# Attention's products in source order on TensorE, V products a block later, projections spread over a pair: a hybrid decoder trunk on one core

## The chip, the cores and the metric

One core of one Trainium2 chip runs the whole kernel in one launch. The metric is the device time of an execution in microseconds; lower is better. Line numbers L... are those of the kernel before, unless a row comes from the changed kernel, where the same lines stand ten to twelve lines further down.

## What is computed

Two layers over 512 positions of width 1024, in float32:

```python
h = rmsnorm(x) * (1 + scale1(c)) + shift1(c)
proj = h @ w_in                      # q, k, v of 3 head groups
# A: 4 heads, two softmax maps each, a = p0 - lam * p1
# B: 6 heads, mixture of 3 dilated windows; C: 6 heads with forget bias
x = x + gate1(c) * (concat(heads) @ w_out)
h = rmsnorm(x) * (1 + scale2(c)) + shift2(c)
u, g = split(h @ w_up)
x = x + gate2(c) * ((silu(conv3(g)) * u) @ w_down)
```

A final rmsnorm follows. scale, shift and gate come from `silu(c) @ w_mod`. Sixteen heads of width 64 make eight pairs.

## The kernel before, in words

**Precision.** Each operand of a large product is held as two parts of a fast matmul type: hi, a copy rounded by ScalarE (ACT), and lo, the rest, taken by VectorE (DVE). A product is three matmuls, hi x hi, hi x lo and lo x hi (`mm3`, L264). Weights are loaded in chunks by SyncE's DMA queue (SP) and split in the same way (L174 on ACT, L186 on DVE); `W.pump` does this one chunk ahead.

**Attention** (`layer_attn`) runs over 64 blocks in each layer: eight pairs in the order B0 B1 A0 C0 A1 C1 B2 C2 (pairs 0 to 7 here), two heads each, four blocks of 128 queries. Block i of a head sees 128 (i + 1) keys. For one block:

- `emit_S`: the score products s (two accumulating matmuls for kinds B and C; kind A has two maps, each in a PSUM buffer of its own, and the pool `ps_s` has two buffers);
- `emit_max` (DVE, L654) adds the mask and takes the row maximum nm; `emit_exp` (ACT, L667); for kind A `emit_norm` combines the two maps;
- `emit_T`: transposes of e into pt (L695); `emit_hi` (ACT, L714) and `emit_lo` (DVE, L719) split them into pth and ptl, once for blocks 0 and 1 of a head together and once each for blocks 2 and 3;
- `emit_PV`: the V products po (L741, L742), four matmuls after block 1 of a head and eight after block 3. `head_post` then forms the head's output: it copies po, divides by the sums through transposes pr, and for kind A normalises with a product sbps.

The loop over b at L819 issues, per step, the transposes of block b - 2, the maximum and exponential of b, the score of b + 1 and the V product of b - 2.

**Fills.** Between these, `fill` puts other products: the q and k projections of the next pair (`qk_chunk`, 24 matmuls of 512 columns each), half a chunk of V projection (`v_half`, 48 matmuls of 256 columns, pairs 0 to 5), and in pair 7 the output projection (`out_part`). `fills` holds their cost per pair; a step of the loop asks for the shares f1, f2 and f3 of it at three places. With 0.06 + 0.055 + 0.055 = 0.17 a step, a pair's fills are used up in about six of its eight blocks. q comes first, then k, then V.

**From a projection to scores.** `qk_post` turns the PSUM result into the tiles qk that the score products read. Kind C copies straight from PSUM (`stack_gen`: L436, L447 on ACT, L433 on DVE). Kind B first applies the rotary tables: a copy qf (ACT, L469), two DMAs that swap neighbouring rows into sw (L471, L472), three DVE operations (L475, L477, L479), then the stack copies with one more ACT copy (L449). Kind A rotates likewise, splits qf into hi (in sw, L254) and lo (in qf, L256), and twelve DMAs on SP's queue (L490) put 32-row pieces into four qk tiles; the first head needs the first six. These steps are generators that `tick` advances one step at a time, with each piece of a fill.

**What orders the instructions.** The source order gives each instruction a priority; a scheduler then places the instructions on each engine by when it expects their inputs. So PE's order before differs from the source: where a score product is not expected to be ready, later products go ahead of it. At run time each engine works through its own list in order.

Of the kernel before, what the change touches and what calls it, by code (L numbers as in the profile page):

```python
# [30 lines left out]
def kernel(  # L31
# [27 lines left out]
    V, A, T, G = nc.vector, nc.scalar, nc.tensor, nc.gpsimd  # L59
# [25 lines left out]
    def tick():  # L85
        for g in list(aux):
            if next(g, StopIteration) is StopIteration:
                aux.remove(g)
# [6 lines left out]
    ident = cst[:, C_ID:C_ID + 128]  # L95
# [20 lines left out]
    for l in range(DEPTH):  # L116
# [16 lines left out]
        for m in range(KC):  # L133
            for b in range(0, FC, 8):
                n = min(8, FC - b)
# [123 lines left out]
    def pair_tiles(pool, tag, name):  # L259
        hi = pool.tile([128, SEQ], F32R, tag=tag, name=name + "h")  # L260
        lo = pool.tile([128, SEQ], F32R, tag=tag, name=name + "l")
        return hi, lo

    def mm3(ps, w, rhs, first, last, c=slice(0, SEQ)):  # L264
        T.matmul(ps[:, c], w[0], rhs[0][:, c], start=first, stop=False, skip_group_check=True)  # L265
        T.matmul(ps[:, c], w[0], rhs[1][:, c], start=False, stop=False, skip_group_check=True)  # L266
        T.matmul(ps[:, c], w[1], rhs[0][:, c], start=False, stop=last, skip_group_check=True)  # L267

    def feat_q(ps, w, act, first=True, last=True, k0=0):
        n = len(act)  # L270
# [108 lines left out]
    def layer_attn(l, ap, mods, st, rt0):  # L379
        h = st.h  # L380
# [5 lines left out]
        def v_post(q, cols):  # L386
            vv = vvs[q]
            for t in range(2):
                src = [cols(2 * t + b).rearrange("p (h d) -> p h d", h=4) for b in range(2)]
                for b in range(2):  # L390
                    A.activation(out=vv[:, 2 * t + b, :, 0:64], in_=src[b], func=AF.Copy)
                yield
                for b in range(2):
                    V.tensor_tensor(out=vv[:, 2 * t + b, :, 64:128], in0=src[b],
                                    in1=vv[:, 2 * t + b, :, 0:64].bitcast(F32), op=ALU.subtract)
                yield
# [4 lines left out]
        def v_half(q, half):  # L401
            nb, n = (1, VZ) if q == 0 else (2, 256)
            if half == 0:
                pools = {"m": (mm, "mm"), "t": (ps_t, "pt"), "o": (ps_o, "o")}
                vps[q] = [pools[c][0].tile([128, SEQ], F32, tag=pools[c][1], name="vps")
                          for c in ("otmt" if q == 0 else "mm")]
            pss = vps[q]
            w = W.use()
            for j in range(4):
                k = 4 * half + j  # L410
                wc = w(n * j, n * j + n)
                for tb in range(4):
                    b = slice(128 * tb, 128 * tb + 128)
                    d = pss[tb // nb][:, 256 * (tb % nb):256 * (tb % nb) + n]
                    go = k == 0 and tb % nb == 0
                    en = k == KC - 1
                    T.matmul(d, h[k][0][:, b], wc[0], start=go, stop=False, skip_group_check=True)
                    T.matmul(d, h[k][0][:, b], wc[1], start=False, stop=False, skip_group_check=True)
                    T.matmul(d, h[k][1][:, b], wc[0], start=False, stop=en, skip_group_check=True)
                W.pump(j)  # L420
                yield
            if half == 1:
                if q == 0:
                    for tb in range(4):
                        V.tensor_tensor(out=z[:, tb, :], in0=pss[tb][:, 256:VZ], in1=fb[:, l, :], op=ALU.add)
                vvs[q] = ap.tile([128, 4, 4, 128], F32R, tag="vv", name="vv", bufs=2)
                aux.append(v_post(q, lambda tb: pss[tb // nb][:, 256 * (tb % nb):256 * (tb % nb) + 256]))
# [86 lines left out]
        def after(g):  # L514
            while True:
                with tc.issue_after(anchor[0]), tc.issue_after(anchor[1]):
                    if next(g, StopIteration) is StopIteration:
                        return
                yield
# [104 lines left out]
        def emit_S(b):  # L624
            idx, kind, hh, i = blocks[b]
            q, k = qks[idx, 0], qks[idx, 1]
            n = 128 * (i + 1)
            qb = slice(128 * i, 128 * i + 128)
            if kind != "A":
                s = ps_s.tile([128, SEQ], F32, tag="s", name="s")  # L630
                T.matmul(s[:, 0:n], q[hh][:, qb], k[hh][:, 0:n], start=True, stop=False)
                if kind == "B":
                    T.matmul(s[:, 0:n], q[hh][:, qb], k[2 + hh][:, 0:n], start=False, stop=True)  # L633
                else:
                    T.matmul(s[:, 0:n], q[2 + hh][0:68, qb], k[2 + hh][0:68, 0:n], start=False, stop=True)
                S[b] = [s]
                return
            res = []
            for mp in range(2):
                s = ps_s.tile([128, SEQ], F32, tag="s", name="s")  # L640
                T.matmul(s[:, 0:n], q[2 * hh + mp][0:96, qb], k[2 * hh + mp][0:96, 0:n], start=True, stop=True)
                res.append(s)
            S[b] = res

# [41 lines left out]
        def emit_T(b):  # L686
            i = blocks[b][3]
            e = E.pop(b)
            if i == 1:
                pt = pts[b - 1][0]  # L690
            else:
                pt = ps_t.tile([128, SEQ], F32, tag="pt", name="pt")
            for j in range(i + 1):
                c = 128 * (i + j) if i < 2 else 128 * j
                T.transpose(pt[:, c:c + 128], e[:, 128 * j:128 * j + 128], ident)  # L695
            if i % 2 == 0:
                n = (384, 1024)[i // 2]
                pts["cur"] = tuple(ap.tile([128, n], F32R, tag="%s%d" % (t, i), name=t, bufs=1) for t in ("pth", "ptl"))
            pts[b] = (pt,) + pts["cur"]
# [21 lines left out]
        def emit_PV(b):  # L721
            idx, kind, hh, i = blocks[b]
            if i % 2 == 0:
                return
            half = i // 2
            _, pth, ptl = pts.pop(b)
            pts.pop(b - 1)
            if half == 0:
                po_t["cur"] = ps_o.tile([128, SEQ], F32, tag="o", name="po")
            po = po_t["cur"]  # L730
            while running("v_post"):
                tick()
            vv = vvs[idx // 2]
            hd = 2 * (idx % 2) + hh
            nj = 2 * half + 2
            for j in range(nj):
                c0 = 128 if j == nj - 1 else 0
                oc = slice(256 * half + c0, 256 * half + 256)
                a = 256 * j if half == 0 else 256 * j + c0
                pc = slice(a, a + 256 - c0)  # L740
                T.matmul(po[:, oc], vv[:, j, hd, :], pth[:, pc], start=(j == 0), stop=False, skip_group_check=True)  # L741
                T.matmul(po[:, oc], vv[:, j, hd, :], ptl[:, pc], start=False, stop=(j == nj - 1), skip_group_check=True)  # L742
            if half == 1:
                aux.append(head_post(idx, kind, hh, po))

# [56 lines left out]
        nb = len(blocks)  # L802

        def running(name):
            return any(g.__name__ == name for g in aux)

        def ready(b):
# [5 lines left out]
            while not done(idx):  # L813
                tick()

        emit_S(0)
        lag = 2
        f1, f2, f3 = 0.06, 0.055, 0.055
        for b in range(nb + lag):  # L819
            idx = blocks[min(b, nb - 1)][0]  # L820
            while idx and fills[idx - 1][0]:
                fill(idx - 1, 1.0)
            p = b - lag
            if l == 0 and b == 10:
                with tc.issue_after(anchor[0]), tc.issue_after(anchor[1]):
                    prep()
            if b == 3:
                aux.append(after(fz_post()))
            if p >= 0:
                emit_T(p)  # L830
            if b < nb:
                emit_max(b)
            if p >= 0:
                emit_hi(p)
            fill(idx, f1)
            if b < nb:
                emit_exp(b)
            if p >= 0:
                emit_lo(p)
            fill(idx, f2)  # L840
            if b + 1 < nb:
                ready(b + 1)
                emit_S(b + 1)
            if b < nb:
                emit_norm(b)
            fill(idx, f3)
            if p >= 0:
                emit_PV(p)
            ms, mr = 4, 3.2
            if b >= ms:  # L850
                for _ in range(int((b - ms + 1) * mr) - int((b - ms) * mr)):
                    next(modg, None)
        aux.append(modg)
        for idx in range(8):
            while fills[idx][0]:
# [137 lines left out]
    with ExitStack():  # L993
# [7 lines left out]
        with tc.tile_pool(name="start", bufs=1) as stp:  # L1001
# [19 lines left out]
            for op in STARTUP:  # L1021
# [4 lines left out]
                else:  # L1026
                    k = int(op[1])
# [162 lines left out]
```

## Time and profile before

| what | value |
|---|---|
| median of three executions | 1338.51 us (1336.86 to 1346.54) |
| profiled execution | 1337.11 us, span 1335.3 us, mean granted clock 0.989 |
| layer 0 attention, blocks | about 60 to 305 us |
| layer 0 MLP | about 310 to 700 us |
| layer 1 attention, blocks | about 700 to 910 us |
| layer 1 MLP and final norm | about 915 to 1335 us |

How to read it: PE is the matmul unit and PEld its weight loads. A row of a timeline has the start and the duration in us; matmuls are pipelined, so a row's duration is longer than the distance to the next start. A row of the table by stretches has the stretch, its length, the busy time of PE, PEld, DVE, ACT and POOL with counts, the granted clock of TensorE, the DMA share and GB/s. A row of the table of waits has who waited for whom, the sum in us, the number and the longest. A row of groups ends with the busy time, the mean ns of one, and the idle time of the engine before them with what ended most of it.

### The profile page before, as it was taken

To read this page: it belongs to the slowest core of one execution; us is meant where nothing else is said; L and a number is where in the kernel's file an instruction comes from. 1 tells how busy PE (TensorE), PEld (TensorE's weight loads), DVE (VectorE), ACT (ScalarE), POOL (GpSimd) and SP (SyncE) were. 2 spreads that over 40 slices of the span, in tenths; PEclk is the share of its full clock that TensorE was granted. 3 is DMA by queue.
4 is the path that set the end of the run, shared out by engine and by line. 5 is a ranking of instruction groups with operands and counts; after the bars stand their busy time and mean duration, and the time that the engine had idled before them with its cause. 6 is when DMAs were issued, how large, how long until landed. Compare 5 with 4: busy or idle time off the path is not lost.

```text
span 1335.3 us, 18235 instructions
## 1 busy us (share of the span) xinstructions
PE 1278.1 (96%) x6568; PEld 1058.2 (79%) x6568; DVE 868.8 (65%) x1733; ACT 671.5 (50%) x1254; POOL 94.1 (7%) x64
## 2 busy tenths in 40 slices
PE   4899999999999999999999999999999999999997
PEld 1688787778888878888898888878878888888886
DVE  6888989868888886433347787875754444443232
ACT  5577888954433333322336677785543333333231
POOL 5232423400000000000000000000000000000000
PEclk8899999999999999999999999999999999999999
DMA  9445553432777775333333234212133333332331
GB/s 373 146 136 158 165 156 129 137 113 82 249 251 256 247 253 152 91 97 93 113 113 94 85 108 128 78 57 89 49 108 95 97 94 96 95 91 87 103 99 63
DMA packets 68127, 174.44 MB, mean 131 GB/s; under 512 B 9410, under 2 KB 11730, under 8 KB 68036
## 3 DMA queue, kind: packets, MB, share of 16 engines
q1 hardware_dynamic: 66884, 172.16, 40.9%
q8 instruction: 52, 0.85, 0.3%
q10 hardware_dynamic: 1088, 1.05, 0.2%
q14 instruction: 39, 0.32, 0.1%
q0 software_dynamic: 64, 0.06, 0.0%
HBM read 159.41 MB, written 2.10 MB: 121 GB/s over the span
## 4 chain that ended last, share of the span: by engine, by line
PE 59%; DVE 9%; DMA 6%; ACT 4%; issue 2%; SPq 0%; DVEq 0%; ACTq 0%
PE dps L265 6%; PE dps L267 6%; PE dps L266 6%; DMA rawm<-in_wmod_dram 5%; PE pg L266 4%; PE pu L265 4%; PE pg L267 4%; PE pu L267 4%; PE pu L266 4%; PE pg L265 4%; DVE wlo L186 2%; PE ops L265 2%; PE ops L266 2%; PE ops L267 2%; DVE rawm L228 2%
## 5 line engine op out<-in xcount | busy, mean ns | idle before, releaser
L186 DVE TENSOR_TENSOR wlo<-raww,whi 128x1024 fp32r<-128x1024 f32 (+3 forms) x188 | 228.2, 1214 | 232.0 <-ACT whi L174 227.8
L174 ACT ACTIVATE whi<-raww 128x1024 fp32r<-128x1024 f32 (+3 forms) x188 | 194.5, 1035 | 335.8 <-PE dps L266 137.8
L266 PE MATMUL pg<-hl,whi 128*128 128x512 f32 (+1 forms) x368 | 143.1, 389 | 0.5 <-DVE hl L314 0.2
L265 PE MATMUL pg<-hh,whi 128*128 128x512 f32 (+1 forms) x368 | 141.5, 385 | 1.6 <-ACT whi L174 1.6
L265 PE MATMUL pu<-hh,whi 128*128 128x512 f32 (+1 forms) x368 | 142.3, 387 | 0.0
L267 PE MATMUL pg<-hh,wlo 128*128 128x512 f32 (+1 forms) x368 | 141.0, 383 | 1.1 <-DVE wlo L186 1.1
L267 PE MATMUL pu<-hh,wlo 128*128 128x512 f32 (+1 forms) x368 | 140.6, 382 | 0.1
L266 PE MATMUL pu<-hl,whi 128*128 128x512 f32 (+1 forms) x368 | 140.7, 382 | 0.0
L265 PE MATMUL dps<-mh,whi 128*128 128x512 f32 x308 | 121.5, 394 | 0.0
L267 PE MATMUL dps<-mh,wlo 128*128 128x512 f32 x308 | 121.5, 394 | 0.0
L266 PE MATMUL dps<-ml,whi 128*128 128x512 f32 x308 | 121.2, 393 | 0.0
L667 ACT ACTIVATE e<-e,nm 128x256 f32<-128x256 f32 (+3 forms) x160 | 88.9, 556 | 33.9 <-DVE nm L654 30.6
L265 PE MATMUL qkps<-hh,whi 128*128 128x512 f32 x224 | 95.7, 427 | 1.0 <-ACT qf L469 0.7
L907 ACT ACTIVATE y<-y 128x512 f32<-128x512 f32 x44 | 27.8, 632 | 127.0 <-DVE y L904 117.0
L266 PE MATMUL qkps<-hl,whi 128*128 128x512 f32 x224 | 89.5, 400 | 0.0
L267 PE MATMUL qkps<-hh,wlo 128*128 128x512 f32 x224 | 89.4, 399 | 0.0
L654 DVE CUSTOM_DVE_ANT_0 e<-s,cst 128x256 f32<-128x256 f32 (+3 forms) x160 | 76.3, 481 | 17.7 <-PE s L633 6.2
L267 PEld LDWEIGHTS pg<-hh,wlo 128*128 128x128 f32 x368 | 69.0, 188 | 17.0 <-DVE wlo L186 2.4
L221 POOL TENSOR_TENSOR rawm<-rawm,scb 128x512 f32<-128x512 f32 x48 | 71.2, 1492 | 160.1 <-DMA rawm<-in_wmod_dram 115.6
L267 PEld LDWEIGHTS pu<-hh,wlo 128*128 128x128 f32 x368 | 69.1, 188 | 16.7 <-DVE wlo L186 1.2
L266 PEld LDWEIGHTS pg<-hl,whi 128*128 128x128 f32 x368 | 69.0, 188 | 16.6 <-DVE hl L314 2.0
L265 PEld LDWEIGHTS pg<-hh,whi 128*128 128x128 f32 x368 | 69.1, 188 | 16.0 <-ACT whi L174 2.0
(183 smaller groups left out, 2820.2 us busy)
## 6 DMA issues: line engine op xcount, KB each, us to landing
raww<-in_wup_dram SPq DMA_DIRECT2D x88, 512.0 KB
rawm<-in_wmod_dram SPq DMA_DIRECT2D x160, 256.0 KB
raww<-in_wqk_dram SPq DMA_DIRECT2D x32, 512.0 KB
raww<-in_wdown_dram SPq DMA_DIRECT2D x32, 512.0 KB
mu<-in_wmod_dram SPq DMA_DIRECT2D x16, 512.0 KB
raww<-in_wout_dram SPq DMA_DIRECT2D x16, 448.0 KB
raww<-in_wv_dram SPq DMA_DIRECT2D x12, 512.0 KB
raww<-in_wdown_dram SPq DMA_DIRECT2D x16, 384.0 KB
```

Of the source, the lines that this page charges most:

```text
L174: A.activation(out=h[:, 0:m], in_=self.raw[i][:, c:c + m], func=AF.Copy)
L186: V.tensor_tensor(out=lo[:, 0:m], in0=raw[:, c:c + m], in1=h[:, 0:m].bitcast(F32), op=ALU.subtract)
L221: G.tensor_tensor(out=raw, in0=raw, in1=scb[:, 512 * half:512 * half + 512], op=ALU.mult)
L228: V.tensor_tensor_reduce(out=raw, in0=raw, in1=scb[:, 512 * half:512 * half + 512], scale=1.0, scalar=prev, op0=ALU.mult, op1=ALU.add, acc ...
L265: T.matmul(ps[:, c], w[0], rhs[0][:, c], start=first, stop=False, skip_group_check=True)
L266: T.matmul(ps[:, c], w[0], rhs[1][:, c], start=False, stop=False, skip_group_check=True)
L267: T.matmul(ps[:, c], w[1], rhs[0][:, c], start=False, stop=last, skip_group_check=True)
L654: anchor[0] = V.tensor_tensor_reduce(out=e[:, 0:n], in0=s[:, 0:n], in1=cst[:, mask + SEQ - n:mask + SEQ], scale=-scale, scalar=3e38, op0=A ...
L667: anchor[1] = A.activation(out=e[:, 0:n], in_=e[:, 0:n], func=AF.Exp, bias=nm, scale=-1.0, accum_out=den).ins
L907: last_silu[0] = A.activation(out=y, in_=y, func=AF.Silu).ins
```

## The change

Three edits, all in `layer_attn` and its helpers:

1. Within the block loop each matmul and transpose of projections, scores, transposes and V products is tied behind the one issued before it (`tc.issue_after`), so PE gets them in source order. `head_post` and `fz_post` still issue their few matmuls untied.
2. `emit_PV` is called for block p - 1 instead of p: one block later; the loop runs one step longer.
3. f1, f2, f3 are 0.045, 0.04, 0.04, together 0.125: one eighth of a pair's fills per block.

```diff
+    row = [False, None]
+
+    def pe(ins):
+        with (tc.issue_after(row[1]) if row[0] and row[1] else ExitStack()):
+            r = ins()
+        row[1] = r.ins
+
+    def mmul(*a, **k):
+        pe(lambda: T.matmul(*a, **k))
+
     def mm3(ps, w, rhs, first, last, c=slice(0, SEQ)):
-        T.matmul(ps[:, c], w[0], rhs[0][:, c], start=first, stop=False, skip_group_check=True)
+        mmul(ps[:, c], w[0], rhs[0][:, c], start=first, stop=False, skip_group_check=True)
...
-                T.transpose(pt[:, c:c + 128], e[:, 128 * j:128 * j + 128], ident)
+                pe(lambda: T.transpose(pt[:, c:c + 128], e[:, 128 * j:128 * j + 128], ident))
...
-        f1, f2, f3 = 0.06, 0.055, 0.055
-        for b in range(nb + lag):
+        f1, f2, f3 = 0.045, 0.04, 0.04
+        row[0] = True
+        for b in range(nb + lag + 1):
...
-            if p >= 0:
+            if 0 <= p < nb:
                 emit_T(p)
...
-            if p >= 0:
-                emit_PV(p)
+            if p >= 1:
+                emit_PV(p - 1)
...
+        row[0] = False
```

The other `T.matmul` calls of `v_half`, `emit_S` and `emit_PV` become `mmul` in the same way.

**Order on PE, start of pair 2 (kind A) in layer 0.** s is a score product, vps the V projection, qkps the q and k projections, pt transposes. Before:

```order
L265 MATMUL qkps<-hh,whi 128x512
L266 MATMUL qkps<-hl,whi 128x512
L267 MATMUL qkps<-hh,wlo 128x512
L641 MATMUL s<-qk 128x128
L265 MATMUL qkps<-hh,whi 128x512
L266 MATMUL qkps<-hl,whi 128x512
L267 MATMUL qkps<-hh,wlo 128x512
```

Now:

```order
L272 MATMUL po<-ptl,vv 128x128
L705 MATMUL pt<-cst,e 128x128 x2
L272 MATMUL vps<-whi,hh 128x256
L272 MATMUL vps<-wlo,hh 128x256
L272 MATMUL vps<-whi,hl 128x256
...
L272 MATMUL s<-qk 128x128 x2
L705 MATMUL pt<-cst,e 128x128 x3
L272 MATMUL qkps<-hh,whi 128x512
```

Before, fifteen qkps matmuls of the next pair's projection and other work stood ahead of the pair's first score product. Now the k projection of this pair is followed by 48 vps matmuls, the scores of blocks 6 and 7 of the pair before, eight po matmuls and three transposes, and then by the score product; the next pair's qkps come behind it. Pairs 1 and 3 to 6 of both layers start in the same way (pair 1 with the pf products and four transposes of the forget bias among the rows).

**Order on ACT, the same place, now.** qf and sw are the k side of pair 2, vv<-vps copies the V projection out, pth is the split of the transposes.

```order
L479 ACTIVATE qf<-qkps 128x512
L677 ACTIVATE e,dens<-e,nm 128x384
L224 ACTIVATE rawm,mq<-rawm 128x512
L677 ACTIVATE e,dens<-e,nm 128x512
L224 ACTIVATE rawm,mq<-rawm 128x512
L759 ACTIVATE ot<-po 64x512
L724 ACTIVATE pth<-pt 128x384
L401 ACTIVATE vv<-vps 128x4x64
L254 ACTIVATE sw<-qf 128x512
```

The split sw<-qf stands behind pth, which reads the two transposes above, and behind a vv copy of the last V projection. At pair 4 of both layers the same two stand ahead of it; at pair 2 of layer 1 only pth does. At pair 6 the stack copies stand behind pth in the same way.

**Order on PE, start of pair 7 (kind C) in layer 0, now.** The qkps here are the k projection of pair 7 itself; ops is the output projection.

```order
L705 MATMUL pt<-cst,e 128x128 x2
L272 MATMUL qkps<-hh,whi 128x512
L272 MATMUL qkps<-hl,whi 128x512
L272 MATMUL qkps<-hh,wlo 128x512
L272 MATMUL qkps<-hh,whi 128x512
L272 MATMUL qkps<-hl,whi 128x512
L272 MATMUL qkps<-hh,wlo 128x512
L272 MATMUL s<-qk 128x128 x2
L705 MATMUL pt<-cst,e 128x128 x3
L272 MATMUL ops<-oh,whi 128x512
```

Before, fourteen other PE rows (V products, the last score of pair 6, transposes, two ops matmuls) stood between the last k projection and that score product; now none does.

More of the change, by code (lines that the diff above doesn't have):

```diff
@@ L262, in pair_tiles @@
         return hi, lo
+    row = [False, None]
[5 more added lines that the diff above has]
+        pe(lambda: T.matmul(*a, **k))
     def mm3(ps, w, rhs, first, last, c=slice(0, SEQ)):
-        T.matmul(ps[:, c], w[0], rhs[0][:, c], start=first, stop=False, skip_group_check=True)
-        T.matmul(ps[:, c], w[0], rhs[1][:, c], start=False, stop=False, skip_group_check=True)
-        T.matmul(ps[:, c], w[1], rhs[0][:, c], start=False, stop=last, skip_group_check=True)
+        mmul(ps[:, c], w[0], rhs[0][:, c], start=first, stop=False, skip_group_check=True)
+        mmul(ps[:, c], w[0], rhs[1][:, c], start=False, stop=False, skip_group_check=True)
+        mmul(ps[:, c], w[1], rhs[0][:, c], start=False, stop=last, skip_group_check=True)
     def feat_q(ps, w, act, first=True, last=True, k0=0):
@@ L416, in v_half @@
                     en = k == KC - 1
-                    T.matmul(d, h[k][0][:, b], wc[0], start=go, stop=False, skip_group_check=True)
-                    T.matmul(d, h[k][0][:, b], wc[1], start=False, stop=False, skip_group_check=True)
-                    T.matmul(d, h[k][1][:, b], wc[0], start=False, stop=en, skip_group_check=True)
+                    mmul(d, h[k][0][:, b], wc[0], start=go, stop=False, skip_group_check=True)
+                    mmul(d, h[k][0][:, b], wc[1], start=False, stop=False, skip_group_check=True)
+                    mmul(d, h[k][1][:, b], wc[0], start=False, stop=en, skip_group_check=True)
                 W.pump(j)
@@ L630, in emit_S @@
                 s = ps_s.tile([128, SEQ], F32, tag="s", name="s")
-                T.matmul(s[:, 0:n], q[hh][:, qb], k[hh][:, 0:n], start=True, stop=False)
+                mmul(s[:, 0:n], q[hh][:, qb], k[hh][:, 0:n], start=True, stop=False)
                 if kind == "B":
-                    T.matmul(s[:, 0:n], q[hh][:, qb], k[2 + hh][:, 0:n], start=False, stop=True)
+                    mmul(s[:, 0:n], q[hh][:, qb], k[2 + hh][:, 0:n], start=False, stop=True)
                 else:
-                    T.matmul(s[:, 0:n], q[2 + hh][0:68, qb], k[2 + hh][0:68, 0:n], start=False, stop=True)
+                    mmul(s[:, 0:n], q[2 + hh][0:68, qb], k[2 + hh][0:68, 0:n], start=False, stop=True)
                 S[b] = [s]
@@ L640, in emit_S @@
                 s = ps_s.tile([128, SEQ], F32, tag="s", name="s")
-                T.matmul(s[:, 0:n], q[2 * hh + mp][0:96, qb], k[2 * hh + mp][0:96, 0:n], start=True, stop=True)
+                mmul(s[:, 0:n], q[2 * hh + mp][0:96, qb], k[2 * hh + mp][0:96, 0:n], start=True, stop=True)
                 res.append(s)
@@ L740, in emit_PV @@
                 pc = slice(a, a + 256 - c0)
-                T.matmul(po[:, oc], vv[:, j, hd, :], pth[:, pc], start=(j == 0), stop=False, skip_group_check=True)
-                T.matmul(po[:, oc], vv[:, j, hd, :], ptl[:, pc], start=False, stop=(j == nj - 1), skip_group_check=True)
+                mmul(po[:, oc], vv[:, j, hd, :], pth[:, pc], start=(j == 0), stop=False, skip_group_check=True)
+                mmul(po[:, oc], vv[:, j, hd, :], ptl[:, pc], start=False, stop=(j == nj - 1), skip_group_check=True)
             if half == 1:
@@ L832, in layer_attn @@
                 emit_max(b)
-            if p >= 0:
+            if 0 <= p < nb:
                 emit_hi(p)
@@ L837, in layer_attn @@
                 emit_exp(b)
-            if p >= 0:
+            if 0 <= p < nb:
                 emit_lo(p)
@@ L846, in layer_attn @@
             fill(idx, f3)
-            if p >= 0:
-                emit_PV(p)
+            if p >= 1:
+                emit_PV(p - 1)
             ms, mr = 4, 3.2
```

## The prediction

> **What bounds the kernel now.** I read the page's busy line first, then a table by stretches for the two attention stages (layer 0: 60 to 305 us, layer 1: 700 to 910), then the table of waits inside them.
>
> ```profile
> span 1335.3 us, 18235 instructions
> PE 1278.1 (96%) x6568; PEld 1058.2 (79%) x6568; DVE 868.8 (65%) x1733; ACT 671.5 (50%) x1254; POOL 94.1 (7%) x64
> ```
> ```profile
> 60.00:305.00 245.00, 230.29 (x1357) 193.13 (x1357) 208.37 (x500) 194.69 (x459) 71.36 (x49) 0.99 0.46 146
> 700.00:910.00 210.00, 205.60 (x1269) 176.06 (x1268) 166.79 (x422) 153.46 (x344) 0.00 (x0) 0.99 0.29 87
> ```
>
> PE sets the end. No matmul is added or removed, so only the time in which PE stands still can change, and the edit works in attention. There PE is idle for 245.00 - 230.29 = 14.7 us and 210.00 - 205.60 = 4.4 us, 19.1 in all. DVE is busy 85% of the first stretch and 79% of the second, so it is no bound by itself. What ends the idle time (the first five rows are layer 0, the last is layer 1):
>
> ```profile
> PE po L742 <- DVE ptl L719: 2.5, 4, 0.8
> PE po L741 <- DVE op L754: 2.3, 2, 2.0
> PE s L641 <- DVE nm L654: 2.0, 3, 1.0
> PE ops L266 <- DVE ol L256: 1.5, 1, 1.5
> PE pt L695 <- DVE e L682: 1.0, 2, 0.8
> ```
> ```profile
> PE pt L695 <- ACT e L667: 1.0, 3, 0.4
> ```
>
> V products (po) and transposes (pt) that come too close behind the exponentials and the splits make up about half of it; no single wait is over 2.0 us.
>
> A wait can also cost clock:
>
> ```profile
> 265.70:269.10 3.40, 1.87 (x8) 1.14 (x7) 3.40 (x6) 1.51 (x5) 3.40 (x3) 1.00 0.24 77
> 269.10:272.50 3.40, 3.40 (x13) 2.97 (x13) 2.56 (x6) 1.94 (x4) 0.58 (x1) 0.51 0.41 132
> ...
> 740.20:743.60 3.40, 3.40 (x13) 2.82 (x11) 3.07 (x12) 3.30 (x9) 0.00 (x0) 0.50 0.41 142
> ```
>
> In the stretch with the 1.5 us wait for ol, PE was busy 1.87 of 3.40 us, and the next 3.4 us ran at a granted clock of 0.51: another 1.7 us lost. The second dip, at 740, comes behind the small pf products of 6 columns (their rows are below). Outside attention's edges these two are the only ones.
>
> **What the change can take away.** A V product one block later, and blocks of equal length, leave the splits about 3 us more. The ceiling: the 19.1 us of idle time, plus some 0.16 us for each of about 37 waits (a 128x512 product is on record for 0.39 us but its successor starts 0.23 us later, rows at 107.54 below, so the idle column leaves out 0.16 of each wait), 5.9, plus the two clock dips, 3.4. Sum 28.4 us. The po and pt waits are some 10 us of idle time and 3.5 us of these tails; the waits of s, ops and the projections have other causes, of which I give a third. I take 18 away; the bounds are 5 and 28.
>
> **What the strict queue adds.** The new PE order puts the first score product of a pair at a fixed place, and everything behind it waits with it. Ahead of it stands the chain that turns the pair's k projection into qk tiles. The trace shows that chain for pair 2 of layer 0 (kind A): the last two projection products, the split on ACT, the fifth and sixth of the twelve copies on SP's queue, the first score product.
>
> ```profile
> 107.54 0.39 PE L266 MATMUL qkps<-hl,whi 128*128 128x512 f32 x1
> 107.77 0.40 PE L267 MATMUL qkps<-hh,wlo 128*128 128x512 f32 x1
> 115.47 0.64 ACT L254 ACTIVATE sw<-qf 128x512 fp32r<-128x512 f32 x1 [0.22 <-DVE qf L479]
> 118.76 1.17 SPq L490 DMA_DIRECT2D qk<-sw  x2
> 119.98 0.58 SPq L490 DMA_DIRECT2D qk<-qf  x1
> 122.62 0.22 PE L641 MATMUL s<-qk 96*128 96x128 f32 x1
> ```
> ```profile
> 816.88 1.79 DMA qk<-sw
> ```
>
> From 108.17 to 122.62 is 14.45 us. Today that costs nothing: PE does V products and then the next pair's projection meanwhile. In the new order only this stands between the same two rows: 48 V projections, the scores of blocks 6 and 7, eight V products, three transposes. Their prices, start to start, from a stretch that has them in a row:
>
> ```profile
> 733.80 0.28 PE L417 MATMUL vps<-whi,hh 128*128 128x256 f32 x1
> ...
> 735.22 0.34 PE L631 MATMUL s<-qk 128*128 128x384 f32 x1
> ...
> 735.57 0.29 PE L741 MATMUL po<-pth,vv 128*128 128x256 f32 x1
> ...
> 736.47 0.30 PE L695 MATMUL pt<-cst,e 128*128 128x128 f32 x1
> 736.52 0.48 PE L631 MATMUL s<-qk 128*128 128x512 f32 x1
> ...
> 737.07 0.28 PE L550 MATMUL pf<-z,cst 128*128 128x6 f32 x2
> ...
> 739.21 0.42 PE L695 MATMUL pt<-cst,e 128*128 128x128 f32 x2
> ```
>
> Twelve V projections take 1.42 us, so 48 take 5.7; scores 0.35 and 0.55; eight V products 0.90; transposes 0.2. That is 7.7 us against a chain of 14. For pairs 1 and 6 the chain is shorter but so is the cover; for pair 7 there is no cover, since its k projection is the last thing before its first score product. I work each hold out from the new ACT order, with these durations:
>
> ```profile
> L714 ACT ACTIVATE pth<-pt 128x384 fp32r<-128x384 f32 x32 | 15.6, 486 | 4.2 <-PE pt L695 3.7
> L436 ACT ACTIVATE qk<-qf 64x512 fp32r<-64x512 f32 x12 | 7.4, 627 | 8.7 <-DVE qf L479 8.6
> L447 ACT ACTIVATE qk<-qkps 64x512 fp32r<-64x512 f32 x12 | 7.1, 593 | 0.3
> L436 ACT ACTIVATE qk<-qkps 64x512 fp32r<-64x512 f32 x12 | 7.1, 589 | 0.2
> L174 ACT ACTIVATE whi<-raww 128x896 fp32r<-128x896 f32 x7 | 6.6, 948 | 3.7 <-PE ops L266 3.7
> L391 ACT ACTIVATE vv<-vps 128x256 fp32r<-128x256 f32 x16 | 5.2, 378 | 1.3 <-PE vps L419 1.1
> ```
>
> Zero is the end of PE's last product ahead of the held score product.
>
> - Pairs 2 and 4, kind A: the split of qf now stands on ACT behind pth (which needs the last two transposes, 1.4 us before zero) and, in three of the four cases, behind a vv copy (which needs products that end 0.7 us before zero). Copy done at -0.17, split done at 0.46, six copies issued at 0.62 apart by 4.2, landed 1.8 later: a hold of 6.0. Without the vv copy 5.4. Four such pairs in two layers: 23.4 us. Bounds per pair: 4.9 (split right behind the transposes) and 14.45 - 7.7 = 6.75.
> - Pair 1, kind B: the stack copies stand behind pth and the small copy after the pf products; the cover is 7.7 us and 2.1 of pf products (737.07 to 739.21). The second score product needs two 0.63 us copies, a 1.05 us weight split and a third copy: 2.3 us each, 4.6. Pair 6, kind B: pth, then five 0.63 us copies behind the last transposes, 2.5 each, 5.0. Bounds 0.5 and 5, the upper one from the 14.8 us of today's chain of pair 1, below, less the cover.
> - Pair 7, kind C, no cover: 0.2 + 0.59 + 0.95 + 0.59, so 2.5 in layer 0 (a weight split stands between), 1.5 in layer 1, 4.0. Bounds 1.5 and today's 3.65.
> - Pairs 3 and 5, kind C: today's 3.65 us of chain against 7.7 of cover, nothing. If the cover were gone they would cost what pair 7 does.
>
> ```profile
> 77.46 0.39 PE L267 MATMUL qkps<-hh,wlo 128*128 128x512 f32 x1
> ...
> 92.65 0.33 PE L633 MATMUL s<-qk 128*128 128x128 f32 x1 [0.73 <-ACT qk L449]
> ```
> ```profile
> 893.16 0.39 PE L267 MATMUL qkps<-hh,wlo 128*128 128x512 f32 x1
> ...
> 897.20 0.33 PE L631 MATMUL s<-qk 128*128 128x128 f32 x1 [0.28 <-ACT qk L447]
> ```
>
> Holds: 23.4 + 4.6 + 5.0 + 4.0 = 37.0 us; bounds 27 and 51. Behind the held product stand the transposes of the block before last, the next pair's projection and all later scores. DVE's maxima and ACT's exponentials hang on those, so both engines can finish what is queued in a hold, but nothing runs ahead.
>
> **Clock.** A hold of 6 us empties a whole 3.4 us stretch, so each kind A pair should bring a dip: 4 x 1.7 = 6.8. A hold of about 2 us brings one only where it falls whole into one stretch, so for the other six I take 2.5 dips, 4.2. Together 11; bounds 0 and 17. [...]
>
> **Small ones.** Kind A uses both score buffers in each block, and the next score products need both maxima done:
>
> ```profile
> L654 DVE CUSTOM_DVE_ANT_0 e<-s,cst 128x384 f32<-128x384 f32 x20 | 10.9, 548 | 2.3 <-PE s L635 1.4 <-PE s L633 0.6
> ...
> L654 DVE DVE_READ_ACCUMULATOR2_ANT nm<- 128x1 f32 x80 | 6.4, 79 | 0.0
> ```
>
> Two of 0.63 us are 1.3, and in source order as little as twelve V projections and a transpose, 1.5 us, lie between two blocks. With DVE 85% busy some come late: 2 us more than today, bounds 0 and 8. The wait for ol, 1.5 us, stays: the output projection's last step still follows right behind the pr transposes. The DMA queues carry the same transfers in nearly the same order; nothing for that.
>
> **Sum.** 37 + 11 + 2 - 18 = +32 us on the profiled execution of 1337.1 us (span 1335.3 and 1.8 around it), 1369. The median of the three runs, 1338.5, is 1.4 above that execution: 1370.
>
> **Rivals.** A measurement of this kernel tells about 1% from no change, 13 us.
>
> - Even pace drains the queues (faster). If DVE and ACT are so relieved that the qk chain ends inside its cover, holds at pairs 1 to 6 vanish. It decides at a kind A chain of 7.7 us instead of 14.45. Then 4 us at pair 7 stand against 28 saved: 1338 - 24 = 1314. Against it: six issues and a landing are 5.5 us alone, and the split itself has been queued behind late PE work. 6%.
> - Catch-up pays (within 1%). Holds as computed at their lower bound, 27, but DVE catches up in them, all 28 us of waits go, and a few dips add 4: 1342. For it: DVE's 208 us of 245 in layer 0. Against it: layer 1, with the same holds, has only 4.4 us of idle time to give back. 16%.
> - Waits stay inside the blocks (slower still). Only 5 us go, all ten holds bring dips (17), kind A's scores wait at their bound (8): 37 + 17 + 8 - 5 = +57, 1395. 18%.
> - That the edit does nothing: ruled out, the order of PE's instructions differs all through attention.
>
> **Chances.** The forecast has 60%, and its own range is 1352 to 1388. 1345 to 1395 leaves out the faster case, the lower part of the catch-up case and the upper part of the last. Faster by over 1%: 0.06; within: 0.16; slower: 0.78.
>
> **What would show it.** Right: in the waits of PE, s <- DMA qk rows of 5 to 7 us at pairs 2 and 4 of both layers, s <- ACT qk of 1.5 to 3 us at pairs 1, 6 and 7; granted clock near 0.5 just behind the long ones; the po rows almost gone; attention stretches of some 258 and 227 us for 245 and 210. Wrong: no wait over 3 us ahead of s, or the po and pt waits still there, or the holds present and the time still unchanged.

## The result, and the profile after

The changed kernel takes 1399.46 us (median of four executions, 1399.11 to 1403.83) where the kernel before takes 1340.67 (1336.86 to 1346.54). The ratio is 1.0446, with a 95% interval of 1.0421 to 1.0472: slower by 60 us. The forecast was 1370 and its range ended at 1395. The direction and the place were right, the size was not. One execution of the run e11 below took 4360.16 us and is left out of its ratio.

The busy line of the page of the changed kernel:

```profile
span 1397.8 us, 18224 instructions
PE 1292.1 (92%) x6568; PEld 1077.4 (77%) x6568; DVE 875.3 (63%) x1733; ACT 671.5 (48%) x1254; POOL 92.6 (7%) x64
```

The same 6568 matmuls, and 18224 instructions in all for 18235: the profile shows no work that the tie itself adds. The span is 62.5 us longer. PE is busy 14.0 us more (1292.1 for 1278.1), which with the same matmuls I put down to the clock (e5 below tests it), and idle 48.5 us more (105.7 for 57.2). Where: the table by stretches, from the first score product of a layer to its last V product, of the kernel before and then of the changed one. The columns are the stretch, its length, busy time of PE, PEld, DVE, ACT and POOL, the granted clock, the DMA share and GB/s.

```profile
64.75:286.45 221.70, 206.99 (x1231) 173.15 (x1230) 192.12 (x474) 182.74 (x442) 70.61 (x49) 0.99 0.47 145
717.68:924.44 206.76, 202.36 (x1219) 171.71 (x1219) 163.08 (x409) 152.13 (x341) 0.00 (x0) 0.99 0.30 91
```
```profile
63.80:308.55 244.75, 209.85 (x1220) 180.29 (x1219) 193.51 (x475) 182.05 (x442) 69.53 (x49) 0.94 0.42 131
746.45:983.50 237.05, 209.97 (x1218) 181.81 (x1219) 165.75 (x408) 151.55 (x340) 0.00 (x0) 0.93 0.26 79
```

Attention takes 23.0 us more in layer 0 and 30.3 in layer 1, 53 of the 62.5. PE's idle time there was 14.7 and 4.4 and is 34.9 and 27.1. The rest lies outside: output-projection matmuls that stood inside these stretches now stand behind them (3.5 us in each layer), and layer 0's MLP is 3.2 us longer (the pu row below). What PE waits for, from the table of waits over the whole run (who for whom, sum in us, number, longest):

```profile
PE s L272 <- DMA qk<-qf: 14.1, 6, 4.3
PE s L272 <- ACT qk L457: 13.7, 6, 3.4
...
PE s L272 <- ACT qk L459: 8.0, 6, 2.3
...
PE s L272 <- DVE nm L664: 6.3, 8, 2.3
...
PE qkps L272 <- ACT qf L479: 5.4, 6, 1.3
PE s L272 <- DMA qk<-sw: 4.7, 1, 4.7
PE s L272 <- DVE dens L769: 4.5, 1, 4.5
PE ops L272 <- ACT oh L254: 2.9, 2, 1.4
PE pr L777 <- ACT dx L772: 2.4, 2, 1.2
PE pu L272 <- DVE wlo L186: 2.4, 4, 1.2
```

The rows of s <- qk, with the one put down to dens (the first score product of pair 4 in layer 1, whose copies were on their way too), are the holds at the pair starts, 45.0 us. No row of po is left. One hold in full, the start of pair 2 in layer 0, from the timeline (start, duration, what; in brackets the idle time before and what ended it):

```profile
118.12 0.41 PE L705 MATMUL pt<-cst,e 128*128 128x128 f32 x2
...
119.08 0.49 ACT L724 ACTIVATE pth<-pt 128x384 fp32r<-128x384 f32 x1
...
119.46 0.38 ACT L401 ACTIVATE vv<-vps 128x256 fp32r<-128x256 f32 x1
...
119.65 0.28 PE L272 MATMUL vps<-whi,hl 128*128 128x256 f32 x1
...
119.73 0.63 ACT L254 ACTIVATE sw<-qf 128x512 fp32r<-128x512 f32 x1
119.77 1.85 SPq L500 DMA_DIRECT2D qk<-sw  x3
...
121.72 0.53 SPq L500 DMA_DIRECT2D qk<-qf  x1
...
124.00 0.30 PE L272 MATMUL s<-qk 96*128 96x128 f32 x1 [4.07 <-DMA qk<-qf]
...
125.91 0.45 PE L272 MATMUL s<-qk 96*128 96x128 f32 x1 [1.62 <-DMA qk<-qf]
```

PE has nothing left to do at 119.93. The split into sw ends at 120.36, 0.43 us later, behind pth and a vv copy. Then come the copies, one after another on SP's queue (by the order of the copies in the source, the first of the three in the row at 119.77 still belongs to the q side), and PE stands 4.07 us, then 1.62 more for the second map's product.

The clock, in stretches of 3.41 us along the same place, and two stretches around the hold of 3.07 us at pair 7:

```profile
118.00:121.40 3.40, 1.93 (x17) 1.73 (x16) 3.10 (x8) 3.35 (x8) 0.00 (x0) 1.00 0.31 74
121.40:124.81 3.41, 0.30 (x1) 0.19 (x1) 2.44 (x7) 0.87 (x4) 0.00 (x0) 1.00 0.39 96
124.81:128.22 3.41, 2.31 (x8) 2.05 (x9) 0.96 (x6) 1.22 (x5) 0.00 (x0) 0.50 0.46 115
128.22:131.63 3.41, 3.41 (x13) 2.83 (x11) 1.56 (x8) 1.10 (x4) 0.00 (x0) 0.50 0.75 190
131.63:135.04 3.41, 3.41 (x21) 2.93 (x20) 2.46 (x8) 1.07 (x2) 1.77 (x2) 1.00 0.97 352
278.30:281.70 3.40, 1.61 (x11) 1.48 (x12) 2.76 (x6) 2.59 (x5) 1.05 (x1) 1.00 0.36 91
281.70:285.10 3.40, 3.40 (x23) 2.96 (x22) 1.38 (x7) 3.37 (x11) 0.22 (x1) 1.00 0.37 124
```

The stretch with 0.30 us of work is followed by half clock. The next one, at half clock, holds the wait for the second map's product, and half clock stays for one more: 6.8 us, not 3.4. The 3.07 us at pair 7 fell across two stretches, each kept 1.6 us of work or more, and no dip followed. In attention 61.0 us run at half clock (27.3 and 33.7), where before it was 6.8.

### The profile page after: what moved, and what is told of

Its sections match the earlier page's. It is cut to its first block, busy times and chain, and to the rows that moved or that the text cites. A ratio compares the mean times of both kernels' runs of the same rounds, so it can differ in the third digit from the quotient of the medians.

```text
span 1397.8 us, 18224 instructions
## 1 busy us (share of the span) xinstructions
PE 1292.1 (92%) x6568; PEld 1077.4 (77%) x6568; DVE 875.3 (63%) x1733; ACT 671.5 (48%) x1254; POOL 92.6 (7%) x64
## 4 chain that ended last, share of the span: by engine, by line
PE 63%; DVE 15%; DMA 10%; ACT 7%; issue 3%; SPq 1%; POOL 0%; DVEq 0%; ACTq 0%; POOLq 0%
PE dps L272 18%; PE pg L272 12%; PE pu L272 12%; PE qkps L272 6%; PE ops L272 6%; DMA rawm<-in_wmod_dram 5%; PE vps L272 3%; DVE wlo L186 2%; PE s L272 2%; DVE rawm L228 2%; PE pt L705 1%; DMA sw<-qf 1%; PE po L272 1%; ACT whi L174 1%; ACT e L677 1%
## 5 line engine op out<-in xcount | busy, mean ns | idle before, releaser
L272 PE MATMUL s<-qk 128*128 128x128 f32 (+11 forms) x256 | 69.1, 342 | 51.3 <-DMA qk<-qf 14.1
L272 PE MATMUL qkps<-hh,whi 128*128 128x512 f32 x224 | 102.8, 459 | 5.4 <-ACT qf L479 5.4
L272 PEld LDWEIGHTS s<-qk 128*128 128x128 f32 (+2 forms) x256 | 50.2, 203 | 67.3 <-ACT qk L457 15.4
L272 PE MATMUL qkps<-hl,whi 128*128 128x512 f32 x224 | 93.2, 416 | 0.0
L272 PE MATMUL qkps<-hh,wlo 128*128 128x512 f32 x224 | 92.6, 413 | 0.0
L272 PEld LDWEIGHTS pg<-hh,wlo 128*128 128x128 f32 x368 | 69.0, 188 | 17.1 <-DVE wlo L186 2.6
```

The lines of the kernel that those rows point to most:

```text
L272: pe(lambda: T.matmul(*a, **k))
```

## The experiments

Two theories were set against each other after the result. The first: the strict row is the whole cost, and its place is the starts of the pairs. The rival: the even shares or the later V products cost something of their own. Each run is compared with the kernel before on the same chip; ratios have 95% intervals. All diffs are against the changed kernel.

### One edit at a time

**e1_no_tie**: the later V products and the even shares, without the row.

```diff
-        row[0] = True
+        row[0] = False
```

> V products a block later and even shares, but no instruction tied behind another. Theory (the tie is the cost: the held first score product of a pair lets nothing pass): the scheduler again puts the next pair's projection ahead of the held score product, so the holds go; some 5 us over the kernel before, 1346, with at most 3 dips of the clock in attention. Rival A (the even spread is the cost, since a pair's k projection ends later whatever the order): 45 us or more over before, 1385. Rival B (the later V product is the cost): 30 us over, 1370.

1340.79 us, ratio 1.0010 (0.9995 to 1.0026): not to be told from the kernel before. The whole loss goes with that one word.

**e2_tie_only**: the row alone, with V products and shares as before; only pair 7 keeps the change's shares.

```diff
+            f1, f2, f3 = (0.06, 0.055, 0.055) if idx < 7 else (0.045, 0.04, 0.04)
...
-            if p >= 1:
-                emit_PV(p - 1)
+            if p >= 0:
+                emit_PV(p)
```

> The tie alone: V products where they were, shares of the kernel before in pairs 0 to 6 (pair 7 keeps the shares of the change). Theory: the cover between the k projection and the first score product grows from 7.7 to only about 9 us, so most holds stay: 45 us over before, 1385, kind A scores still held 4 to 5 us. Rival A: about 10 us over, 1350. Rival B: 20 us over, 1360.

1421.66 us, 1.0600 (1.0577 to 1.0622): slower than the change itself, where 1385, faster than the change, was expected. Its waits have two large rows that the changed kernel lacks (of four rows of po, 18.1 us in all):

```profile
PE po L272 <- DVE ptl L729: 10.1, 12, 2.1
...
PE po L272 <- ACT pth L724: 6.4, 2, 3.4
```

In a strict row a V product that waits for its splits holds up everything as well.

**e3_spread_only**: the even shares alone (no row, `emit_PV(p)`).

> The even shares alone, without tie and with V products where they were. Theory: as without the tie above, 5 us over before, 1346. Rival A: 45 us over, 1385. Rival B: no change, 1340.

1344.56 us, 1.0037 (1.0020 to 1.0054): a small loss, about what the theory had.

**e4_lag_only**: the later V products alone (no row; shares of before in pairs 0 to 6).

> The later V product alone, no tie, shares of the kernel before in pairs 0 to 6 (pair 7 as in the change). Theory: a few waits of V products go, 3 us under before, 1337. Rival A: the same. Rival B: 30 us over, 1370.

1337.33 us, 0.9975 (0.9960 to 0.9990): 3.4 us faster than the kernel before. Its attention, in the table by stretches:

```profile
64.78:284.40 219.62, 202.53 (x1216) 172.54 (x1215) 193.99 (x473) 178.71 (x441) 68.64 (x49) 0.98 0.47 145
718.67:919.82 201.15, 196.49 (x1204) 168.94 (x1204) 162.21 (x408) 150.83 (x340) 0.00 (x0) 0.99 0.30 91
```

PE is idle for 17.1 and 4.7 us, 21.8 in all, where the kernel before has 19.1. So in this one profile, without the row, giving the splits more time does not lessen PE's idle time: other waits take the place of the po rows (score products wait 7.5 us for maxima where they waited 3.9).

**e8_tie_lag**: the row and the later V products, with the shares of before.

```diff
+            f1, f2, f3 = (0.06, 0.055, 0.055) if idx < 7 else (0.045, 0.04, 0.04)
```

> Tie and later V products with the shares of the kernel before (pair 7 with those of the change). Theory: the V products' waits that the tie alone has (10 us and the clock behind them) go, the holds stay as in the tie alone: 1405. Rival (the even spread is what made the change better than the tie alone): 1420.

1403.87 us, 1.0481 (1.0456 to 1.0506), close to the theory's 1405. Its po rows:

```profile
PE po L272 <- DVE dens L769: 1.5, 2, 1.0
...
PE po L272 <- ACT pth L724: 0.4, 1, 0.4
PE po L272 <- DVE ptl L729: 0.3, 1, 0.3
...
PE po L272 <- DVE op L764: 0.2, 1, 0.2
```

From e2 to e8 the po waits fall from 18.1 us to 2.4, and the time by 1.2%, 16 us. From e8 to the changed kernel the even shares add a gain of 0.35%, some 5 us, hardly more than the two intervals leave open. So the row costs 6.0%, and inside it the other two edits give back a quarter of that. The first theory's main clause stands: the row is the cost. The rival fell as an account of the 4.5%: outside the row the later V products alone are worth -0.25% and the even shares alone +0.37%.

### Where in the row

**e5_filler**: the changed kernel, with 152 dummy products of 512 columns into the score product's own buffer ahead of the held products of nine pair starts; their result is overwritten. Each hold stays about as long, but PE works in it.

```diff
+PAD = {(0, 2): (18, 6), (0, 4): (20, 4), (0, 6): (11, 0), (0, 7): (13, 0), (1, 0): (14, 0), (1, 2): (18, 6),
+       (1, 4): (19, 5), (1, 6): (5, 0), (1, 7): (13, 0)}
...
+                idle(s, pad[mp])
                 mmul(s[:, 0:n], q[2 * hh + mp][0:96, qb], k[2 * hh + mp][0:96, 0:n], start=True, stop=True)
```

> The change, with products of no use put on TensorE ahead of the held score products (4 to 20 of 512 columns at nine of the sixteen pair starts, about as long as each hold was; they go into the score's own buffer and are overwritten). Theory (the holds also drop the clock, and that is some 20 us of the 60): the dips of 6.8 us at pairs 2 and 4 go, at most 5 dips are left in attention, and the time falls by 15 to 20 us to about 1381. Rival (the dips fall into time that is lost anyway, only the holds count): no change, 1399, or a few us more.

1384.34 us, 1.0334 (1.0312 to 1.0356): 15 us less than the changed kernel for 152 products more. Its attention:

```profile
64.16:303.00 238.84, 219.17 (x1290) 188.01 (x1291) 189.22 (x474) 182.35 (x441) 70.59 (x49) 0.98 0.44 135
737.93:966.57 228.64, 216.54 (x1300) 186.71 (x1299) 168.47 (x417) 154.17 (x346) 0.00 (x0) 0.99 0.28 83
```

The granted clock is 0.98 and 0.99 for 0.94 and 0.93: 13.6 us at half clock for 61.0. The holds with products in them lasted as long as before (the first two, at pair 2 of layer 0, 3.97 and 1.42 us for 4.07 and 1.62). So about 15 of the 60 us are half clock behind the holds; this agrees with the 14.0 us more of busy time on the page of the changed kernel.

**e6_late**: the changed kernel, but the first score product of a pair stands in the source behind the transposes and 0.36 of the next pair's projections (0.13 of the output projection in pair 7). The rest of the pair's steps take 0.08 each (0.11 in pair 7).

```diff
-        emit_S(0)
...
-        f1, f2, f3 = 0.045, 0.04, 0.04
+        f1, f2, f3 = 0.03, 0.025, 0.025
...
+            if idx == 7:
+                f1, f2, f3 = 0.04, 0.035, 0.035
...
+            if b < nb and b % 8 == 0:
+                fill(idx, HEAD if idx < 7 else 0.13)
+                ready(b)
+                emit_S(b)
...
-            if b + 1 < nb:
-                ready(b + 1)
+            if b + 1 < nb and (b + 1) % 8:
                 emit_S(b + 1)
```

> The change, still tied, but in the source the first score product of a pair comes behind the transposes of that step and the first 0.36 of the next pair's fills (27 projection products, 6.2 us; 0.13 in pair 7); the other blocks share the rest, 0.08 each. Theory (only the bare pair starts cost): cover at pairs 2 and 4 grows from 7.7 to some 16 us, holds there vanish, a hold of 2 us stays at pair 7, at most 4 dips: 1340, as fast as before or a little faster. Rival (a strict queue costs in every block): 1375 or more, with waits of s and pt spread over all blocks.

1389.05 us, 1.0363 (1.0336 to 1.0391). The holds at the pair starts are gone, all but 3.0 us at pair 7, and the time falls by 11 us only. The other clause of the first theory, that only the pair starts cost, fell here. What has come in their place:

```profile
PE s L272 <- DVE nm L664: 16.3, 14, 2.0
...
PE qkps L272 <- ACT qf L479: 8.4, 6, 1.4
PE pr L777 <- ACT dx L772: 7.8, 6, 2.7
...
PE po L272 <- DVE op L764: 5.3, 2, 3.5
...
PE pf L560 <- DVE dens L769: 3.7, 1, 3.7
```

With 0.08 of the fills between two blocks instead of 0.125, the score product comes before its buffer's maximum is taken (nm, 16.3 us for 6.3 in the changed kernel), the next projection before the copy out of the last one is done (qf, 8.4 for 5.4), the transposes of a head's end before their operand (dx, 7.8 for 2.4). The cover was moved, not made.

**e7_free_s**: the changed kernel with the score products outside the row; projections, transposes and V products stay in it (`True` lets `pe` issue a product untied).

```diff
+            def mmul(*a, **k):
+                pe(lambda: T.matmul(*a, **k), True)
```

> The change, but the score products alone are not tied; projections, transposes and V products still are. Theory: the scheduler puts the first score product of a pair behind up to 18 projections again; 1345. Rival (the strict queue of the other products costs): 1380 or more.

1362.28 us, 1.0177 (1.0148 to 1.0207). 36 of the 60 us go, more than by moving the pair starts, though not all of it: the time lies between the theory's 1345 and the rival's 1380. The largest rows of s that are left:

```profile
PE s L643 <- DVE nm L670: 14.3, 20, 2.5
...
PE s L643 <- ACT qk L459: 4.1, 5, 2.6
```

The waits of s for qk have shrunk from 45.0 us to some 6; those for maxima are almost as long as in e6 and more than twice those of the changed kernel (6.3).

**e9_free_first**: the changed kernel with only the first block's score products of each pair outside the row. The scheduler puts them behind three transposes and up to six projection products.

```diff
+            def mmul(*a, **k):
+                pe(lambda: T.matmul(*a, **k), hh == 0 and i == 0)
```

> The change, but the score products of the first block of each pair are outside the strict row (the other 56 blocks' scores stay in it). The scheduler then puts them behind 3 transposes and up to 6 projection products, about 2 us of cover, without taking fills from other blocks. Theory (what costs is a product that stands too near behind its chain, and the pair starts are the largest such places): holds at pair starts 49 us shrink by about 2 us at each kind A start and 1 us at pairs 1, 6 and 7, about 14 us, and some 6 us of clock with them: 1380 (1374 to 1387). Rival (the scores inside the blocks are what costs, since untying all of them gave back 37 us while moving the pair starts gave only 10): 1393 or more.

1388.78 us, 1.0364 (1.0342 to 1.0385). The holds fall from 45.0 us to 29.1, a little more than the 14 us that were expected, but the time falls by 11 us where 20 were expected. That is just outside the range of the theory and short of the rival's 1393. Of the holds that are left, these rows are put down to other work, but stand at the first score products of pairs 2, 4 and 7:

```profile
PE s L643 <- DVE wlo L186: 5.7, 2, 3.1
...
PE s L643 <- DVE dens L775: 3.2, 1, 3.2
...
PE s L643 <- DMA rawm<-in_wmod_dram: 2.5, 1, 2.5
```

Layer 1's attention is 11 us shorter; layer 0's only 2.6, though its holds fell by 8: the waits of the projection for the copy qf grew there from 2.6 to 4.5 us, those for dx from 1.2 to 3.0, and the time at half clock from 27.3 to 30.7.

**e10_late_a**: e6's edit for pairs 2 and 4 only; the other pairs are as in the change.

```diff
+            f1, f2, f3 = (0.03, 0.025, 0.025) if idx in (2, 4) else (0.045, 0.04, 0.04)
...
+            if b < nb and b in LATE:
+                fill(idx, HEAD)
+                ready(b)
+                emit_S(b)
...
+HEAD, LATE = 0.36, (16, 32)
```

> The change, but only in pairs 2 and 4 the first score product stands in the source behind 0.36 of the next pair's projections; the rest of the pair's blocks then take 0.085 each instead of 0.125. Theory: the four kind A holds of 6.3 us and their half-clock stretches go (25 and about 10 us), and blocks with too little cover give some 15 to 20 us back as waits for the maxima, the transposes' copies and the projection's buffer: about 1383 (1375 to 1391). Rival (cover is a zero sum: what the start takes the blocks lose): 1395 or more. Second rival (only holds cost): 1365.

1388.75 us, 1.0352 (1.0322 to 1.0381), inside the theory's range. The four kind A holds, 23.3 us, are gone, and the time falls by 11 to 13 us. (The profile is of the fastest of its four executions, 1381.20 us.) Part of what came back, from its waits:

```profile
PE s L272 <- DVE nm L664: 9.6, 12, 1.7
...
PE pt L705 <- DVE e L692: 3.8, 4, 2.0
PE pr L777 <- ACT dx L772: 3.2, 3, 1.2
```

Three ways to remove 16, 23 and 42 us of holds (e9, e10, e6) each gave some 11. The theory that is left: in a strict row every product that stands closer behind its inputs than they take is a hold for all of PE. The pair starts are the largest such places (45.0 us in the changed kernel) and their half clock comes with them (61.0 us, and 13.6 with products in the holds), but as long as the row stays, cover that one place gains another loses in part.

### A version that beats both

**e11_best**: no row, V products one block later, shares between those of the two kernels.

```diff
-        row[0] = True
+        row[0] = False
...
+            f1, f2, f3 = (0.05, 0.05, 0.05) if idx < 7 else (0.045, 0.04, 0.04)
```

> No strict row; V products one block later; shares 0.05, 0.05, 0.05 in pairs 0 to 6 and 0.045, 0.04, 0.04 in pair 7, between those of e1 and e4. Theory (without the row neither the shares nor the later V products cost anything that can be told, the scheduler makes the rest): 0.9975 to 1.001 of the time before, 1337 to 1341. Rival (earlier projections are what makes e4 faster than before): a value half way between e4's 0.9975 and e1's 1.0010, so 0.9993, and above e4.

1335.81 us, 0.9967 (0.9954 to 0.9981), a little below the theory's range. The same kernel in a second run, for its trace:

> The kernel of the run before once more, for its trace. Theory: no V product waits for the rounded transposes (in the kernel before, po waits for ptl), no hold over 4 us at a pair start, at most one half-clock stretch in each layer's attention, and 0.995 to 0.999 of the time before. Rival (its 0.9967 was this chip's spread): 0.999 or more.

1335.64 us, 0.9968 (0.9953 to 0.9983): both runs agree, 4 to 5 us faster than the kernel before. Its attention:

```profile
64.53:279.36 214.83, 200.54 (x1216) 170.57 (x1215) 187.18 (x473) 180.06 (x441) 70.78 (x49) 1.00 0.48 148
717.10:919.04 201.94, 196.93 (x1204) 169.81 (x1204) 162.81 (x408) 149.94 (x340) 0.00 (x0) 0.99 0.30 91
```

Idle 14.3 and 5.0 us, about what the kernel before has, 3.4 us at half clock for 6.8, no hold over 1 us at a pair start. Part of the shorter stretches is work that moved behind them, as in the changed kernel. That no V product would wait for ptl was nearly right: one wait of 0.5 us is left of 2.7, and of all po waits 1.5 of 5.9. Whether it differs from e4 (0.9975) can't be told: the intervals overlap.

## Why the prediction was off

Point by point, by the sum 37 + 11 + 2 - 18 = +32. The profiled execution shows 62.5.

- **Holds, 37**: measured 45.0 us of idle time (2.2 of it was there before, so +42.8). Kind A, predicted 23.4: 23.3. At pair 2 of layer 0 the split came 0.43 us behind PE's last product where 0.46 was worked out. At pair 2 of layer 1, where the early split was to make the hold 5.4 us, it came 0.94 us behind, held up by DVE's rotation (L489) and not by pth, and the hold was 6.0; the other three were a little shorter than worked out, so that the sum is this close is partly luck. Pair 1: 1.9 for 4.6. Pair 6: 7.0 for 5.0. Pair 7: 6.2 for 4.0. Pairs 3 and 5: none, as predicted. Pair 0, for which the forecast had no term: 6.5. In layer 1, fifteen products of pair 1's projection stood ahead of that first score product; in the strict order they come behind it, and it waits 3.37 us for its ACT copies. In layer 0 the second product waits 2.34. The working was sound in the main; a place was overlooked. (The bounds were added up wrongly: those given for each pair come to 24.6 and 54.3 us, not 27 and 51. The 45.0 lies inside both.)
- **Clock, 11**: 14.0 by the busy line, 15 by e5. Of thirteen dips ten follow a stretch with at most 1.13 us of work, two (at 930 and 968) one with 1.78 and 1.75, and one, at 773, comes behind the small pf products (769.92 to 773.33, busy for all 3.41 us), as one did before. Six and a half dips were counted on, and each kind A hold brought 6.8 us of half clock, not 3.4: the first 3.41 us at half clock, with the second map's wait in them, had 1.58 to 2.31 us of work, and the next 3.41 were at half clock too. Of the shorter holds, the 2.34 us of layer 0's pair 0 lay in one stretch (63.37 to 66.78, 1.07 us of work) and brought a dip. The 3.07 us at pair 7 of layer 0, across two, brought none, while the 3.14 us of layer 1's pair 7 left 0.91 us of work in one (950.83 to 954.24) and did. Only the size was off.
- **Small ones and removed waits, 2 - 18 = -16**: measured +3.4 in PE's idle time of attention outside the pair starts. This is the step that failed: "I take 18 away". The po rows did go, all 5.9 us. But score products waiting for maxima rose from 3.9 to 6.3 us, projections waiting for the copy qf from 0.7 to 5.4 (k stands right behind q in the row, before the copy of q out of PSUM is done), ops and pr from 1.9 to 5.7. Some 19 of the 30 us that were missing lie here. The runs show two reasons. First, these 18 us were not to be had: without the row the later V products gain 3.4 us (e4) and do not lessen the idle time. Second, inside the row they do gain 16 (e2 to e8), but from a state that the forecast had not priced, in which the row alone has 18.1 us of po waits. The ceiling was read from the order of before, in which the scheduler had already let other products pass each product that was late.
- **Outside attention, 0**: +2.3, of which the four waits of pu for a weight split make 2.4.

42.8 + 14.0 + 3.4 + 2.3 = 62.5.

**The rivals.** The even pace did not drain the queues: DVE's share of layer 0's attention fell from 87% to 79%, but the chain's length is SP's six issues and a landing, behind pth and vv. The catch-up rival, 1342, failed for the same reason as the 18 us, and its holds of 27 us were 45.0. "Waits stay inside the blocks", 1395 with 18%, came closest: its +57 had 17 for dips (14 to 15) and nothing much given back, as happened; that its time came so near is partly luck, for it took 37 us for the holds and 8 for the maxima, where 42.8 and 2.4 were measured. It deserved more weight, and the profile had the reason: in layer 1, with the same holds, only 4.4 us of idle time could be given back. "The edit does nothing" was rightly ruled out.

**What would show it**: the rows named for pairs 2 and 4 are there (two waits, 5.7 to 6.0 together), those of pairs 1, 6 and 7 too, though smaller at pair 1 and larger at pair 6; clock 0.50 behind the long ones; the po rows gone. The stretches were to grow by 13 and 17 us and grew by 23 and 30.

What stays open: which of the products still tied in e7 cost its 1.8% was not tried.

## What to carry to other kernels

An order fixed by hand on the engine that sets the end turns each operand that is late by a little into idle time of everything behind it (here PE's idle time went from 57.2 to 105.7 us); before fixing it, list for every product the chain ahead of it and the work that stands between, and count every place where the first is longer, not only the largest. Waits that a trace shows under a scheduler's order are what is left after it has let other work pass (the po waits were 5.9 us before and 18.1 in the row alone); neither take them as a sum that a new order can save, nor as all that a strict order will show. Moving work to cover one wait uncovers another unless the queue has work to spare (42 us of holds went in e6, and 11 us of time), so price a hold's removal by what the next place loses.

## What the runs showed of the hardware

- Half clock followed stretches in which PE was at work for about half of the time. In the changed kernel it was busy 1.78 us of the stretch 926.94 to 930.35 and 1.75 us of 964.48 to 967.90, and the 3.41 us behind each ran at 0.50; in the kernel before the same followed 1.87 us of work (265.70 to 269.10). Behind 1.73 us (278.41 to 281.82) the clock stayed at 1.00. What made the difference the runs do not show. The rows of one such dip, and of the stretch with 1.73 us:

```profile
926.94:930.35 3.41, 1.78 (x11) 1.51 (x12) 1.65 (x6) 3.33 (x7) 0.00 (x0) 1.00 0.00 0
930.35:933.76 3.41, 3.41 (x15) 3.04 (x14) 3.14 (x8) 2.36 (x7) 0.00 (x0) 0.50 0.00 0
278.41:281.82 3.41, 1.73 (x11) 1.60 (x12) 2.88 (x6) 2.60 (x5) 1.17 (x1) 1.00 0.38 94
```

- Half clock lasted 6.8 us behind the kind A holds of the changed kernel: at pair 2 of layer 0 the stretch 124.81 to 128.22 had 2.31 us of work at half clock, and the next, with 3.41, was at half clock again.
- Filling the waits with products of no use paid here: with 152 products more the changed kernel was 15 us faster, with 13.6 us at half clock in attention for 61.0 (e5).
